# Hybrid gated block in fp32 on one core: eight late down-weight sums, late up-weight splits, and squares behind the embedding copies

## Chip, cores and metric

One core of a Trainium2 chip runs one launch of a hand-written kernel. The metric is the device time of that launch in microseconds (us), as the median of several runs. Engines are named as in the profile: PE is TensorE, DVE is VectorE, ACT is ScalarE, POOL is GpSimd, SP is SyncE (it only issues DMAs here). Line numbers L... are those of the kernel before, unless a row of the changed kernel is shown.

## What is computed

A decoder block with batch 1, sequence 512, model width 1024, one layer, all in float32:

```python
h = rms_norm(x, g_mix_pre); z = h @ w_in              # 1024 -> 512 + 1024 + 1024 + 2048
u_pool, u_rx, u_rg, gates = split(z); gate_pool, gate_rnn = sigmoid(gates)
y_pool = pool_mixer(u_pool, pool_w, pool_scale) @ w_pool_out
y_rnn = rg_lru_branch(u_rx, u_rg, ...) @ w_rg_out
x = x + rms_norm((gate_pool * y_pool + gate_rnn * y_rnn) @ w_o, g_mix_post)

up = rms_norm(x, g_ffn_pre) @ w_up                    # 1024 -> 2 * 3072
hid = gelu(causal_dwconv(up[..., :3072], w, b)) * up[..., 3072:]
x = x + rms_norm(hid @ w_down, g_ffn_post)            # 3072 -> 1024

ple_gate = sigmoid(rms_norm(x, g_ple_gate) @ w_ple_gate)
ple = rms_norm(p @ w_ple_proj, g_ple_post)            # the embedding product, 256 -> 1024
out = x + ple_gate * ple
```

The change lies between the product with `w_o` and the product with `w_down`.

## The kernel before

**Products.** A float32 product is made of three matmuls (`mm3`, L222 to L224): each operand is split into a rounded part `hi` and a remainder `lo`, and hi·hi, hi·lo and lo·hi are added in PSUM, a memory of eight banks of 128 x 512. A weight block of 128 x 1024 is loaded by SP into one of six `raw` buffers; ACT rounds it (the *cast*, L195 or L455), DVE subtracts (the *remainder*, L191), and `split` does both. The buffer is free for the next load when the remainder is done. `weight` asks for blocks four products ahead (`AHEAD`).

**Seven products in place of eight.** The products with `w_rg_out`, `w_o`, `w_up` and `w_down` are done over 2 x 2 blocks (two halves of the tokens, two halves of the sum or of the columns) by a scheme of seven products, numbered 1 to 7 and called *forms*. Sums and differences of activation blocks are made by DVE. Those of weight blocks are mostly made in DRAM, by accumulating DMAs that POOL issues (`sum_in_dram`, L303 to L311): for the down weights 48 of them, in 24 blocks that are read back later as `wdsum`. Of the up weights only the first two pairs do that; from the third pair on DVE adds the blocks (`up_form`, L387).

**Stages around the change.** Tokens go in four tiles of 128. First comes the product with `w_o` (forms in the order 1, 2, 5, 6, 3, 7, 4; L1070 to L1096): as a form's bank is done, ACT copies it or DVE subtracts it (L1078, L1086, L1088, L1091). Behind each come `x2_sum` and `x2_out`, which normalise a token tile (two *squares* on ACT with a running sum, L489, a power on POOL, two multiplies on DVE), store `x2` to DRAM and make the inputs of the up product, `h2_tile` transposes them on PE, and ACT and DVE split them again.

Second, `ple_tile(t)` makes the embedding product of token tile t in two banks; DVE copies the one (L833), ACT the other (L834), SP stores both. `ple_norm(t)` takes two squares of the result. Third comes the up product. Its 24 column blocks are done in 12 pairs of one gate block and one value block. Pair 0 is done plainly, with blocks 11, 21, 12, 22 (`up_plain`), pairs 1 to 11 by `up_product(f, p)` in the order 1, 3, 6, 2, 7, 5, 4 (form 3 of pair p comes after form 1 of pair p+1). Their banks are `zb` for forms 1, 6 and 7, `gb` and `ub` for the gate and the value, `db` for form 5. After each of forms 1, 5, 6 and 7 ACT copies the bank with or without a sign (L1125, L1128, L1130, L1132, L1133), and PE goes on accumulating onto what was written. Last comes the down product (`down_product`, 7 forms of 6 blocks, L1337 on), with transposes and the embedding gate behind it.

**What sets the order.** PE runs in program order. On the other engines a list scheduler orders instructions by data and by priority: `urgent()` raises it, `tc.high_priority(offset)` too. `behind(ins, name)` adds an edge that only fixes an order on the engine, without a wait. An instruction waits at the head of its engine's queue, and all behind it wait with it. `paced[0]` is the last copy of ACT; `sum_in_dram(sums, n, paced[0])` makes the next n sums wait for it, so that they are spread over the up product. Before, two sums follow each of forms 1, 6 and 5 of pairs 2 to 9 (from `SUMS_FROM`, `SUMS_AFTER`, `SUMS_EACH`): six per pair, 48 in all.

Of the kernel before, what the change touches and what calls it, by code (L numbers as in the profile page):

```python
# [12 lines left out]
ALU = mybir.AluOpType  # L13
# [35 lines left out]

UP_SUMS = (1, 2)  # L50

SUMS_FROM, SUMS_AFTER, SUMS_EACH = 2, (1, 6, 5), 2


PLACES, PLACE_UP, PLACE_H2 = 64, 48, (1072, 46)
# [28 lines left out]
def block_kernel(  # L84
# [62 lines left out]
    def parts_of(n):  # L147

        return [wpool.tile([P, D], F32R, tag=t, name=nm(t))[:, :n] for t in ("hi", "lo")]
# [4 lines left out]
    def behind(ins, name):  # L154
        tc.add_manual_dep(
            ins.ins,
            name,
            mybir.DependencyInfo(mybir.DependencyClass.NoSync, mybir.DependencyReason.DATA),
            reason="order on the engine",
        )  # L160
# [46 lines left out]
    def row(a):  # L207
        return a.rearrange("p (a b) -> p a b", a=2)
# [178 lines left out]
    def up_form(p, f):  # L387

        b = blocks
        if p == 0:  # L390
            t = block(0, f)
        elif p in UP_SUMS:
            t = block(p, {1: 11, 2: 21, 3: 22}.get(f, f))
        elif f == 1:
            for k in (11, 12, 22, 21):
                b[p, k] = block(p, k)
            b[p, 0] = wpool.tile([P, 2, S], F32, tag="sum", name=nm("sum"), bufs=1)
            t = b[p, 11]
        elif f == 6:
            add(b[p, 0], b[p, 11], b[p, 12])  # L400
            t = b[p, 11]
            add(t, b[p, 0], b[p, 22])
        elif f == 7:
            t = b[p, 12]
            add(t, t, b[p, 22])
        elif f == 4:
            t = b[p, 21]
            add(t, b[p, 11], t)
        else:
            t = b[p, {2: 21, 3: 22, 5: 0}[f]]  # L410
        hi, lo = (v.rearrange("p (j c) -> p j c", j=2) for v in parts_of(D))
        split(hi, lo, t)
        if p == 0 and PLAIN.index(f) > 1:
            behind(last_copy[0], h2f_done[0])
        if p == 0 and PLAIN.index(f) > 0:
            behind(last_sub[0], h2n_done[1])
        if p == 1 and f != 1:
            behind(last_copy[0], h2_done[0])
        if (p, f) == (1, 4):
            behind(last_sub[0], hid_done[0])  # L420
        if p > 2 and f == 6:
            behind(last_copy[0], z_done[0])
        ready["up", p, f] = (hi, lo)

    def prep(key):
        if key[0] == "up" and key not in parts:
# [392 lines left out]

    rp = {}  # L820
    h2n_done, h2f_done, z_copied, hid_done, summed = {}, [None], [None], [None], {}

    def ple_tile(t):
        pair = []
        for h in range(2):
            w = weight(("wpp", h))
            ps = bank()
            for k in range(2):
                a = pick(pq[k], t * P, (t + 1) * P)
                mm3(ps, a, pick(w, k * S, (k + 1) * S), k == 0, k == 1)  # L830
            pair.append(ps)
        outs = [slot(), slot()]
        V.tensor_copy(row(outs[0]), back(pair[0]))  # L833
        ACT.copy(row(outs[1]), back(pair[1]))  # L834
        for h, o in enumerate(outs):
            nc.sync.dma_start(pled[t * P : (t + 1) * P, h * S : (h + 1) * S], o)
        return outs

    def ple_norm(t, outs):
        s = rstd_of(outs, in_order=False)  # L840
        rp[t] = const.tile([P, 1], F32, tag=f"rp{t}", name=f"rp{t}")
        V.tensor_copy(rp[t], s)

# [33 lines left out]
    def o_form(f):  # L877

        h11, h12, h21, h22 = (halves(mq[k], b) if k < len(mq) else None for b in range(2) for k in range(2))
        v = {1: h11, 2: h12, 4: h22}.get(f)  # L880
        if f in (5, 7):
            od[f] = quad("C", F32)[:, 0:2, :].rearrange("p a (b c) -> p (a b) c", b=2)
        if f == 5:
            v = od[5]
            behind(V.tensor_tensor(v, h21, h22, ALU.subtract), last_low[0])
        elif f == 6:
            v = od[5]
            V.tensor_tensor(v, v, h11, ALU.subtract)
        elif f == 3:
            v = od[5]  # L890
            V.tensor_tensor(v, v, h12, ALU.add)
        elif f == 7:
            v = od[7]
            V.tensor_tensor(v, h11, h21, ALU.subtract)
        of[f] = quad("A").rearrange("p (s a) (b c) -> p s (a b) c", s=2, b=2)
        split(of[f][:, 0], of[f][:, 1], v)
        if f in (2, 5):
            behind(last_copy[0], z_copied[0])

    def o_lhs(f, k, i):  # L900
        v = of[f][:, :, k, i * P : (i + 1) * P]
# [168 lines left out]
    for n, f in enumerate(SERIAL):  # L1070
        banks = {1: oz, 2: o11, 5: od5, 6: oz, 3: o12, 7: oz, 4: oz}[f]
        last = f == SERIAL[-1]
        for q in product("wo", o_lhs, f, banks, f in (1, 5), tail=2 if f in (1, 6, 3, 7, 4) else 0):
            if q in (0, 2) and n + 1 < len(SERIAL) and SERIAL[n + 1] not in of:
                o_form(SERIAL[n + 1])
            if f == 1:
                with urgent():
                    z_copied[0] = ACT.copy(o11[q - 2], oz[q - 2]).ins.name  # L1078
            if f == 7 and q == 2:
                x2_norm(1, (o11[1], o12[1]))  # L1080
            if last and q == 2:
                h2_tile(0)
        for i in range(2):
            with urgent():
                if f == 5:
                    ACT.copy(o5[:, i], od5[i])  # L1086
                elif f == 6:
                    V.tensor_tensor(o12[i], o5[:, i], oz[i], ALU.subtract)  # L1088
                elif f == 7:
                    with urgent():  # L1090
                        V.tensor_tensor(o5[:, i], o5[:, i], oz[i], ALU.subtract)  # L1091
        if f == 3:
            x2_norm(0, (o11[0], o12[0]))
            for h in range(2):
                h2h.append(token_halves())
                h2l.append(token_halves())  # L1096
# [15 lines left out]
    def up_product(f, p):  # L1112
        for i in range(2):
            w = weight(("up", p, f))
            if f == 1 and p > 1:
                gb[i] = bank()
                if p == 2 and i == 0:
                    PE.matmul(gb[i], w[0][:, 0, :P], w[0][:, 0, :], start=True, stop=True)
            o = {1: zb, 6: zb, 7: zb, 2: gb, 4: gb, 3: ub, 5: {0: db, 1: db}}[f][i]
            a = HALF if f == 4 or (f, i) == (5, 1) else 0  # L1120
            products(o[:, a : a + HALF], w, i, forms[f], f in (1, 5))
            z = zb[i][:, :HALF]
            with urgent():
                if f == 1 and p > 1:
                    paced[0] = ACT.copy(gb[i][:, :HALF], z).ins.name  # L1125
                elif (f, i) == (5, 1):
                    q5[p] = temp()
                    paced[0] = ACT.copy(q5[p], o).ins.name  # L1128
                elif f == 6:
                    paced[0] = ACT.activation(ub[i][:, :HALF], z, AF.Identity, scale=-1.0).ins.name  # L1130
                elif f == 7:
                    ACT.copy(gb[i][:, HALF:], z)  # L1132
                    z_done[0] = ACT.activation(ub[i][:, HALF:], z, AF.Identity, scale=-1.0).ins.name  # L1133
# [12 lines left out]
    def hidden(j, pu, q):  # L1146
# [8 lines left out]
            pu = hid[j]  # L1155
        hid_done[0] = V.tensor_tensor(hid[j], act_g[j], pu, ALU.mult).ins.name

    for t in range(NT):
        with tc.high_priority(offset=3 * URGENT):
            outs = ple_tile(t)  # L1160
        if t == 1:
            h2_tile(1)
            x2_out(2, h2_done[0])
            x2_sum(3, (oz[1], o5[:, 1]))
            x2_out(3)
            ple_norm(0, outs0)
        if t == 0:
            outs0 = outs
        else:
            ple_norm(t, outs)  # L1170
    for kind, n in O_AFTER:
        if kind == "tr":
            h2_tile(n)
# [53 lines left out]
    for p in range(1, NPAIR + 1):  # L1227
        for q, f in seven(p):
            if (q, f) == (1, 1):
                continue  # L1230
            up_product(f, q)
            if f in SUMS_AFTER and p >= SUMS_FROM:
                sum_in_dram(down_sums, SUMS_EACH, paced[0])
            if f == 4:
                for i in range(2):
                    gated_half(2 * q + i, gb[i])
            if f == 3:
                for i in range(2):
                    hidden(2 * q + i, ub[i], q5[q][:, i * HALF : (i + 1) * HALF])
# [94 lines left out]
        )  # L1334
    nq = [None, None]

    for _ in down_product(1, zd, True, tail=2):  # L1337
        pass
    for i in range(2):
        with urgent():  # L1340
            ACT.copy(c11[i], zd[i])
    for _ in down_product(2, c11, False, head=2):
        pass
    for _ in down_product(5, dd, True):
# [146 lines left out]
```

## Time and profile before

| what | value |
|---|---|
| runs | 707.17, 707.8, 709.17 us |
| median | 707.8 us |
| the profiled execution, by its own time | 711.61 us |
| its span in the profile | 709.8 us |
| its mean granted TensorE clock | 0.997 |
| moved by DMA, over the span | 175.72 MB, 248 GB/s mean |

The profiled execution is 3.8 us longer than the median of the other runs; durations are taken from it. How to read its rows: a row of the timeline has the start in us from the start of the span, the duration of one, engine, line, operation, out<-in with the shape, and in brackets how long the engine had been idle and for what. A row that ends in x2 or x3 stands for as many in succession, and its duration is their sum. A row of a group has the busy time in all and the mean of one in ns. A row of windows has the stretch, then the busy us of the engines, the granted clock, the busy share of the DMA engines and GB/s. PE is busy while a matmul is in its pipeline.

### The profile page before, as it was taken

The numbers are of one execution on the slowest core, as the hardware profiler recorded it, in microseconds if no ns is written. First come the engines' busy times: TensorE is split into PE (matmuls) and PEld (weight loads), VectorE is DVE, ScalarE is ACT, GpSimd is POOL, SyncE is SP. The second block draws the span as 40 slices with busy tenths as digits, with TensorE's granted clock in tenths as the row PEclk, the third lists the DMA queues.
The fourth block names the chain that finished last, engine by engine and source line by source line (L and its number), as shares of the span: only waits on it lengthen the run. The fifth ranks groups of instructions, "written<-read, shape, count | busy, mean of one in ns | idle before, by whom it ended". The sixth has DMA issues, their size and how long they took to land.

```text
span 709.8 us, 11608 instructions
## 1 busy us (share of the span) xinstructions
PE 695.8 (98%) x4423; PEld 639.9 (90%) x4423; DVE 592.3 (83%) x772; ACT 454.7 (64%) x693; POOL 94.7 (13%) x123
## 2 busy tenths in 40 slices
PE   9999999999999999999989999999999999999997
PEld 8888888888888998889989999999999888888886
DVE  5698745999759898787979999997999999789972
ACT  6757789835447565579846776665768766665631
POOL 0311321412000000111013222221300000000100
PEclk9999999999999999999999999999999999999999
DMA  8999899999997988764478999997977676868111
GB/s 310 412 304 278 244 237 254 244 289 239 280 336 276 320 328 327 260 239 147 133 244 250 262 309 251 321 233 262 252 202 243 196 265 216 285 212 257 68 61 60
DMA packets 67289, 175.72 MB, mean 248 GB/s; under 512 B 6049, under 2 KB 6689, under 8 KB 66849
## 3 DMA queue, kind: packets, MB, share of 16 engines
q1 hardware_dynamic: 49808, 124.64, 50.1%
q0 software_dynamic: 17280, 50.34, 30.1%
q8 instruction: 35, 0.57, 0.3%
q14 instruction: 22, 0.17, 0.1%
q10 hardware_dynamic: 144, 0.00, 0.0%
HBM read 162.37 MB, written 62.91 MB: 317 GB/s over the span
## 4 chain that ended last, share of the span: by engine, by line
PE 70%; DVE 12%; DMA 8%; ACT 6%; issue 3%; POOL 0%; SPq 0%; DVEq 0%; ACTq 0%
PE ps L222 22%; PE ps L224 22%; PE ps L223 22%; DMA raw<-in_w_up_dram 4%; PE ps L563 3%; DVE lo L191 3%; ACT m L166 1%; DVE m L701 1%; DMA parts<-hi 1%; ACT t L166 1%; DVE m L628 1%; ACT hi L195 1%; DVE t L772 1%; PE ps L672 1%; DMA raw<-in_w_pool_out_dram 1%
## 5 line engine op out<-in xcount | busy, mean ns | idle before, releaser
L191 DVE TENSOR_TENSOR lo<-raw,hi 128x1024 fp32r<-128x1024 f32 (+2 forms) x199 | 230.9, 1187 | 51.1 <-ACT hi L455 30.3
L222 PE MATMUL ps<-A,hi 128*128 128x256 f32 (+1 forms) x672 | 213.0, 317 | 3.7 <-ACT ps L1130 2.8
L223 PE MATMUL ps<-A,hi 128*128 128x256 f32 (+1 forms) x672 | 212.3, 316 | 0.0
L224 PE MATMUL ps<-A,lo 128*128 128x256 f32 (+1 forms) x672 | 212.2, 316 | 0.0
L455 ACT CAST hi<-raw 128x1024 fp32r<-128x1024 f32 (+1 forms) x118 | 118.1, 1012 | 59.1 <-PE ps L224 27.6
L222 PEld LDWEIGHTS ps<-A,hi 128*128 128x128 f32 x672 | 129.0, 192 | 12.4 <-ACT ps L1130 3.0
L224 PEld LDWEIGHTS ps<-A,lo 128*128 128x128 f32 x672 | 129.1, 192 | 6.9
L223 PEld LDWEIGHTS ps<-A,hi 128*128 128x128 f32 x672 | 129.0, 192 | 6.7
L222 PE MATMUL ps<-C,hi 128*128 128x256 f32 x376 | 103.7, 276 | 2.0 <-ACT m L834 2.0
L223 PE MATMUL ps<-C,hi 128*128 128x256 f32 x376 | 103.3, 275 | 0.8 <-DVE C L191 0.8
L224 PE MATMUL ps<-C,lo 128*128 128x256 f32 x376 | 103.2, 274 | 0.0
L195 ACT CAST hi<-raw 128x1024 fp32r<-128x1024 f32 x78 | 80.4, 1051 | 33.2 <-PE ps L223 16.2
L222 PE MATMUL ps<-hi,A 128*128 128x512 f32 x224 | 85.2, 380 | 1.1 <-issue 1.1
L223 PE MATMUL ps<-lo,A 128*128 128x512 f32 x224 | 84.9, 379 | 0.0
L224 PE MATMUL ps<-hi,A 128*128 128x512 f32 x224 | 84.9, 379 | 0.0
L222 PEld LDWEIGHTS ps<-C,hi 128*128 128x128 f32 x376 | 71.8, 191 | 2.7 <-ACT m L834 2.3
L223 PEld LDWEIGHTS ps<-C,hi 128*128 128x128 f32 x376 | 71.8, 191 | 1.2 <-DVE C L191 1.1
L224 PEld LDWEIGHTS ps<-C,lo 128*128 128x128 f32 x376 | 71.8, 191 | 0.0
L484 POOL TENSOR_TENSOR s<-s,mhalf 128x1 f32<-128x1 f32 (+1 forms) x21 | 14.8, 707 | 319.2 <-DVE s L500 297.3
L222 PEld LDWEIGHTS ps<-hi,A 128*128 128x128 f32 x224 | 42.3, 189 | 7.4 <-issue 1.5
L307 POOL DMA_DIRECT2D wdsum<-in_w_down_dram x36 | 33.3, 1086 | 113.1 <-ACT ps L1125 50.1
L224 PEld LDWEIGHTS ps<-hi,A 128*128 128x128 f32 x224 | 42.3, 189 | 6.0
(202 smaller groups left out, 1069.3 us busy)
## 6 DMA issues: line engine op xcount, KB each, us to landing
raw<-in_w_up_dram SPq DMA_DIRECT2D x46, 512.0 KB, 7.2
wdsum<-in_w_down_dram POOLq DMA_DIRECT2D x36, 512.0 KB, 9.0
raw<-in_w_in_dram SPq DMA_DIRECT2D x32, 512.0 KB, 8.7
raw<-wdsum SPq DMA_DIRECT2D x24, 512.0 KB, 4.4
raw<-in_w_down_dram SPq DMA_DIRECT2D x18, 512.0 KB, 3.9
wosum<-in_w_o_dram POOLq DMA_DIRECT2D x12, 512.0 KB, 8.5
wdsum<-wdsum POOLq DMA_DIRECT2D x12, 512.0 KB, 7.9
raw<-wosum SPq DMA_DIRECT2D x8, 512.0 KB, 6.3
```

The lines of the kernel that those rows point to most:

```text
L166: ins = ACT.activation(o, i, func, **kw)
L191: return V.tensor_tensor(o, a, b, ALU.subtract)
L195: last_copy[0] = ACT.copy(hi, src)
L222: PE.matmul(o, ah, bh, start=start, stop=False, **kw)
L223: PE.matmul(o, ah, bl, start=False, stop=False, **kw)
L224: PE.matmul(o, al, bh, start=False, stop=stop, **kw)
L307: ins = nc.gpsimd.dma_start(o, i, **kw)
L455: ins = ACT.copy(hi, raw)
L484: last_pow[0] = nc.gpsimd.tensor_tensor(y, v, mhalf[:, :n], ALU.pow).ins.name
L563: PE.matmul(rx[m], a[:, o : o + P], turns(b), start=k == 0 and i == 0, stop=k == KD - 1 and i == 2)
L628: return V.tensor_tensor(row(o), back(ps), row(rb), ALU.mult)
L672: PE.matmul(ps, bd[pr, a, o], turns(b[pr]), start=i == 0, stop=i == 2)
```

## The change

Five edits, all in the order of work; no arithmetic changes.

1. **Sums of the down weights.** After form 1 two, after forms 6 and 5 one each: four per pair, from pair 2 on as long as there are pairs (2 to 11). Four more wait for the last product of hidden values (`hid_done`), and the last four for the copies of the first form of the down product.
2. **Late up weights.** The splits of blocks 12 and 22 of pair 0 are kept in a list and issued after `h2_tile(1)`, behind the remainders of the second token tile.
3. **Squares of the embeddings.** All four `ple_norm` come after all four `ple_tile`, and their squares go behind the copy L834 of the last tile (`ple_done`). The squares in `x2_out(3)` go behind the copy of tile 2.
4. **Form 3 of the up product**, pairs 2 to 11: the cast of its weight goes behind both form-6 copies of its own pair (`z6_done`).
5. **Product with `w_o`**: the remainders of the activations of forms 7 and 4 go behind the two subtractions after form 6 (`o_done`).

```diff
-SUMS_FROM, SUMS_AFTER, SUMS_EACH = 2, (1, 6, 5), 2
+SUMS_FROM, SUMS_AFTER, SUMS_DOWN = 2, {1: 2, 6: 1, 5: 1}, 4
...
+        if p == 0 and f in PLAIN[2:]:
+            late.append((f, t))
+            return
         hi, lo = (v.rearrange("p (j c) -> p j c", j=2) for v in parts_of(D))
         split(hi, lo, t)
-        if p == 0 and PLAIN.index(f) > 1:
-            behind(last_copy[0], h2f_done[0])
-        if p == 0 and PLAIN.index(f) > 0:
+        if (p, f) == (0, PLAIN[1]):
             behind(last_sub[0], h2n_done[1])
...
+        if p > 1 and f == 3:
+            behind(last_copy[0], z6_done[p])
         ready["up", p, f] = (hi, lo)
+
+    def late_splits():
+        for f, t in late:
+            hi, lo = (v.rearrange("p (j c) -> p j c", j=2) for v in parts_of(D))
+            low = last_low[0]
+            split(hi, lo, t)
+            behind(last_copy[0], h2f_done[0])
+            behind(last_sub[0], low)
+            ready["up", 0, f] = (hi, lo)
...
-        ACT.copy(row(outs[1]), back(pair[1]))
+        ple_done[0] = ACT.copy(row(outs[1]), back(pair[1])).ins.name
...
-    def ple_norm(t, outs):
-        s = rstd_of(outs, in_order=False)
+    def ple_norm(t, outs, after):
+        s = rstd_of(outs, in_order=False, after=after)
...
+        if f in (7, 4):
+            behind(last_sub[0], o_done[f == 4])
...
-                    V.tensor_tensor(o12[i], o5[:, i], oz[i], ALU.subtract)
+                    o_done[i] = V.tensor_tensor(o12[i], o5[:, i], oz[i], ALU.subtract).ins.name
...
-                    paced[0] = ACT.activation(ub[i][:, :HALF], z, AF.Identity, scale=-1.0).ins.name
+                    z6_done[p] = paced[0] = ACT.activation(ub[i][:, :HALF], z, AF.Identity, scale=-1.0).ins.name
...
+        ple_outs.append(outs)
         if t == 1:
             h2_tile(1)
+            late_splits()
             x2_out(2, h2_done[0])
             x2_sum(3, (oz[1], o5[:, 1]))
-            x2_out(3)
-            ple_norm(0, outs0)
-        if t == 0:
-            outs0 = outs
-        else:
-            ple_norm(t, outs)
+        if t == 2:
+            x2_out(3, ple_done[0])
+    for t in range(NT):
+        ple_norm(t, ple_outs[t], ple_done[0])
...
-                sum_in_dram(down_sums, SUMS_EACH, paced[0])
+                sum_in_dram(down_sums, SUMS_AFTER[f], paced[0])
...
+    sum_in_dram(down_sums, SUMS_DOWN, hid_done[0])
     for _ in down_product(1, zd, True, tail=2):
         pass
     for i in range(2):
         with urgent():
-            ACT.copy(c11[i], zd[i])
+            paced[0] = ACT.copy(c11[i], zd[i]).ins.name
+    sum_in_dram(down_sums, None, paced[0])
```

The edits move instructions on ACT at three places. Row names are the kernel's tiles with running numbers, and line numbers of the changed kernel are 13 to 15 higher.

At the embedding copies of token tiles 2 and 3, ACT before (L489 with `m455`, `m456` are the squares of x2 of the last token tile, with `m560` to `m565` those of the first two embeddings; L834 are the copies that free a bank, `C504` and `C506` casts of the last token tile, `hi612` the cast of an up weight):

```order
L195 CAST hi612_3228<-raw611_3226 128x1024
L489 ACTIVATE rb_134,s580_3133<-m455_2652 128x512
L489 ACTIVATE rb_134,s581_3135<-m456_2654 128x512
L489 ACTIVATE rb_134,s586_3145<-m560_3059 128x512
L489 ACTIVATE rb_134,s587_3147<-m561_3060 128x512
L834 COPY m597_3180<-ps595_3172 128x512
L834 COPY m605_3210<-ps603_3202 128x512
L489 ACTIVATE rb_134,s590_3155<-m564_3079 128x512
L195 CAST C504_2881<-ps615_3281 128x4x128
L195 CAST C506_2883<-ps618_3292 128x4x128
L489 ACTIVATE rb_134,s591_3157<-m565_3080 128x512
```

and in the changed kernel, where L847 is the copy, L501 the square, and `hi564` and `hi566` are the two late up weights:

```order
L195 CAST hi564_3095<-raw552_3033 128x1024
L847 COPY m583_3146<-ps581_3138 128x512
L195 CAST hi566_3099<-raw554_3042 128x1024
L195 CAST hi612_3228<-raw611_3226 128x1024
L501 ACTIVATE rb_134,s584_3153<-m455_2652 128x512
L501 ACTIVATE rb_134,s585_3155<-m456_2654 128x512
L847 COPY m593_3180<-ps591_3172 128x512
L195 CAST C504_2881<-ps615_3281 128x4x128
L195 CAST C506_2883<-ps618_3292 128x4x128
L501 ACTIVATE rb_134,s594_3185<-m556_3051 128x512
L1042 COPY m616_3288<-ps615_3281 128x2x128
```

The first copy now stands ahead of all these squares and the second behind only those of x2, two casts of weights have come in, and the squares of the embeddings (from `m556` on) follow the casts of the last token tile.

At form 6 of pair 1, ACT before (`A548` is the input of form 3 of the up product, `ps621` and `ps622` the value banks that L1130 writes, the casts with `hi` are of up weights: `hi653` of form 1 of pair 2, `hi656` of form 3 of pair 1, `hi660` and `hi663` of forms 6 and 2 of pair 2):

```order
L195 CAST A548_3029<-m645_3551 128x512
L195 CAST A548_3029<-m646_3553 128x512
L195 CAST hi650_3569<-raw649_3567 128x1024
L195 CAST hi653_3601<-raw652_3599 128x1024
L195 CAST hi656_3631<-raw655_3629 128x1024
L1130 ACTIVATE ps621_3303<-ps549_3030 128x256
L1130 ACTIVATE ps622_3316<-ps550_3031 128x256
L195 CAST hi660_3663<-raw659_3661 128x1024
L195 CAST hi663_3697<-raw662_3695 128x1024
L1128 COPY t658_3659<-ps551_3032 128x512
```

and in the changed kernel, with L1145 for L1130:

```order
L195 CAST A548_3029<-m645_3551 128x512
L195 CAST hi650_3569<-raw649_3567 128x1024
L195 CAST hi653_3601<-raw652_3599 128x1024
L195 CAST A548_3029<-m646_3553 128x512
L195 CAST hi656_3631<-raw655_3629 128x1024
L195 CAST hi660_3663<-raw659_3661 128x1024
L1145 ACTIVATE ps621_3303<-ps549_3030 128x256
L1145 ACTIVATE ps622_3316<-ps550_3031 128x256
L195 CAST hi663_3697<-raw662_3695 128x1024
L1143 COPY t658_3659<-ps551_3032 128x512
```

One more cast, `hi660`, stands ahead of the two copies, and half of the cast of `A548` goes behind two casts of weights.

At form 6 of pair 2, ACT before (`hi686` is the weight of form 3 of that pair, `hi683` that of form 1 of the next):

```order
L195 CAST hi683_3849<-raw678_3840 128x1024
L1130 ACTIVATE ps621_3303<-ps549_3030 128x256
L195 CAST hi686_3879<-raw685_3877 128x1024
L1130 ACTIVATE ps622_3316<-ps550_3031 128x256
L1132 COPY ps670_3741<-ps549_3030 128x256
L1133 ACTIVATE ps621_3303<-ps549_3030 128x256
```

and in the changed kernel:

```order
L195 CAST hi683_3848<-raw678_3839 128x1024
L1145 ACTIVATE ps621_3303<-ps549_3030 128x256
L1145 ACTIVATE ps622_3316<-ps550_3031 128x256
L195 CAST hi686_3878<-raw685_3876 128x1024
L1147 COPY ps670_3741<-ps549_3030 128x256
L1148 ACTIVATE ps621_3303<-ps549_3030 128x256
```

The cast that stood between the two copies now stands behind them; the same edge is set in every pair from 2 to 11.

More of the change, by code (lines that the diff above doesn't have):

```diff
@@ L821, in block_kernel @@
     h2n_done, h2f_done, z_copied, hid_done, summed = {}, [None], [None], [None], {}
+    z6_done, o_done, ple_done, late = {}, {}, {}, []
     def ple_tile(t):
@@ L1156, in hidden @@
         hid_done[0] = V.tensor_tensor(hid[j], act_g[j], pu, ALU.mult).ins.name
+    ple_outs = []
     for t in range(NT):
```

## The prediction, made before the changed kernel was run

> **What bounds the kernel now.** The page first: which engine is full.
>
> ```profile
> PE 695.8 (98%) x4423; PEld 639.9 (90%) x4423; DVE 592.3 (83%) x772; ACT 454.7 (64%) x693; POOL 94.7 (13%) x123
> ```
>
> TensorE is busy for 695.8 of 709.8 us and its matmuls are untouched by the change, so all that can be won is in its few waits. The view of waits, TensorE's own, from 270 to 520 us, lists them whole (waited for: us in total, times, longest):
>
> ```profile
> PE ps L222 <- ACT ps L1130: 2.8, 1, 2.8
> PE ps L222 <- ACT m L834: 2.0, 1, 2.0
> PE ps L222 <- issue: 1.1, 1, 1.1
> PE ps L222 <- ACT ps L1125: 0.8, 1, 0.8
> PE ps L223 <- DVE C L191: 0.8, 1, 0.8
> ```
>
> Five stops, 7.6 us. Two come with a hidden price, which the windows show (columns of the first: PE, PEld, DVE, ACT, POOL busy, clock, DMA share, GB/s; of the others PE alone, clock, DMA):
>
> ```profile
> 330.00:340.00 10.00, 10.00 (x92) 10.00 (x91) 10.00 (x15) 7.23 (x13) 0.00 (x0) 1.00 0.46 157
> 360.00:370.00 10.00, 7.17 (x64) 1.00 0.66 225
> 370.00:380.00 10.00, 10.00 (x76) 0.83 0.54 185
> 372.00:373.00 1.00, 1.00 (x6) 0.50 0.93 324
> 322.00:323.00 1.00, 1.00 (x11) 1.00 0.84 311
> ```
>
> At full clock 92 of the 256-wide matmuls pass in 10 us, 0.11 us each. After the 2.8 us stop the granted clock is 0.50 and 76 pass in the next ten: 16 are missing, 1.7 us. After the 2.0 us stop (322:323) it is 1.00, nothing more is lost. [...]
>
> **The change part by part.** Three edits lie in front of 330 us.
>
> ```profile
> 283.84 0.45 PE L222 MATMUL ps<-hi,A 128*128 128x512 f32 x1 [1.14 <-issue]
> 281.91 1.23 DVE L191 TENSOR_TENSOR A<-C,A 128x1024 fp32r<-128x1024 f32 x1 [0.21 <-ACT A L195]
> 283.05 1.29 DVE L1088 TENSOR_TENSOR ps<-sum,ps 128x512 f32<-128x512 f32 x2
> 312.62 0.38 PE L223 MATMUL ps<-C,hi 128*128 128x256 f32 x1 [0.78 <-DVE C L191]
> 308.49 3.47 DVE L191 TENSOR_TENSOR lo<-raw,hi 128x1024 fp32r<-128x1024 f32 x3
> 321.05 0.38 PE L222 MATMUL ps<-C,hi 128*128 128x256 f32 x1 [2.04 <-ACT m L834]
> 319.05 0.63 ACT L489 ACTIVATE rb<-m 128x512 f32<-128x512 f32 x1
> 320.43 1.05 ACT L834 COPY m<-ps 128x512 f32<-128x512 f32 x2
> ```
>
> First, the subtraction at L1088, which the product after it accumulates onto, moves ahead of two remainders of 1.23 us that are not yet due: its first half can run when its bank is done, before 282.7, and the 1.14 us stop goes (1.2 with the restart). Second, two of the three remainders at 308.49 are the late up weights (1.13 us each); put behind the second token tile they let that tile's own remainder start 2.3 us earlier, more than the 0.78 us wait (0.9). Third, the squares of the embedding norms (0.73 us each on ACT, with the read of the sum) go behind the copies that free the banks, and the copy of tile 2 now stands before the squares of the last token tile: the 2.04 us wait goes (2.1). Together 4.2 us.
>
> ```profile
> 310.35 1.97 SPq L379 DMA_DIRECT2D raw<-up1sum  x3
> ```
>
> On SP these three loads, issued back to back now, come apart: four stores of embeddings and two of x go between them. Their products start after 330, and the loads of the whole run take 7.2 us or less in the median (row below), so I cost this at nothing; without that cover it would be the wait of one load. POOL keeps its order; its sums only wait for later copies of ACT.
>
> I don't expect TensorE to keep them. The squares are not fewer, only later, and the next token tile's casts stand behind them:
>
> ```profile
> 323.30 1.28 DVE L191 TENSOR_TENSOR C<-ps,C 128x512 fp32r<-128x512 f32 x2
> 327.72 1.07 ACT L195 CAST C<-ps 128x512 fp32r<-128x512 f32 x2
> 339.03 0.36 ACT L1185 COPY ps<-ps 128x256 f32<-128x256 f32 x1 [1.56 <-DVE t L1140]
> 345.39 2.94 ACT L195 CAST hi<-raw 128x1024 fp32r<-128x1024 f32 x3
> 348.24 0.64 ACT L1130 ACTIVATE ps<-ps 128x256 f32<-128x256 f32 x2
> 348.82 0.28 PE L222 MATMUL ps<-A,hi 128*128 128x256 f32 x1
> ```
>
> Today four squares lie between the remainder of token tile 2 (323.30) and the casts of tile 3 (327.72); in the new order six, 1.5 us more. Adding the rows along ACT and DVE in the new order, that remainder comes 2.2 us earlier (1.2 from the first stop, the rest from the two remainders moved away), so the casts come only about half a us earlier, while TensorE wants them 4.2 us earlier: it stops there for some 2 us, and for about 0.6 us before that on banks that the copies between those squares free. DVE is full behind them (10.00 in 330:340), and there one remainder of a weight now stands ahead of the second step of L1140, for which L1185 waits at 339.03: its lead stays near 0.5 us. Last, ahead of L1130 now stand four casts instead of three. They take 0.95 each (2.85 from 345.39 to 348.24), so L1130 starts at 348.24 + 0.95 - 0.5 = 348.7, ends 0.3 later, and TensorE, which starts the product behind it at 348.82 now, starts it near 349.0. So by 349 the 4.2 us are gone, to within 0.2 us; I put this stage at 0. Its ends: without any lead on ACT 349.2 + 0.3, a loss of 0.7; with the lead of all three stops, a gain of 4.2 less 0.95, 3.2.
>
> The part with a lasting effect is a line that is easily missed: the cast of a later weight (form 3, used five products on) is put behind both copies of form 6.
>
> ```profile
> 358.45 1.23 DVE L385 TENSOR_TENSOR sum<-raw,raw 128x1024 f32<-128x1024 f32 x1 [2.01 <-DMA raw<-in_w_up_dram]
> 360.26 1.22 DVE L191 TENSOR_TENSOR lo<-raw,hi 128x1024 fp32r<-128x1024 f32 x1
> 361.54 6.87 DMA raw<-in_w_up_dram
> 363.70 0.37 ACT L1130 ACTIVATE ps<-ps 128x256 f32<-128x256 f32 x1
> 364.38 0.69 DVE L1149 TENSOR_TENSOR h<-ps,t 128x512 f32<-128x512 f32 x1
> 368.48 1.04 ACT L195 CAST hi<-raw 128x1024 fp32r<-128x1024 f32 x1 [4.41 <-DMA raw<-in_w_up_dram]
> 369.43 0.37 ACT L1130 ACTIVATE ps<-ps 128x256 f32<-128x256 f32 x1
> 369.85 0.38 PE L222 MATMUL ps<-A,hi 128*128 128x256 f32 x1 [2.83 <-ACT ps L1130]
> ```
>
> The remainder at 360.26 frees the buffer of a load of 6.87 us; the cast that waits for it (368.48) stands between the two copies of L1130, and TensorE waits for the second. In the new order that copy needs only DVE's L1149 (364.38 + 0.69), so it can run at 365.1, 1.9 us before TensorE stops at 367.0 (369.85 - 2.83). Besides, the remainder goes ahead of the sum that waits 2.01 us for DMA, so the load leaves earlier too. What is queued behind the waiting cast on ACT are then L1132 and L1133. Even with the load as late as today they would follow at 369.4, and the product that needs them starts 12 and then 24 matmuls after 367.0, at 371. So this stop falls whole: 2.8, and the 1.7 of half clock.
>
> The sums: six issues in each pair from the second to the ninth become four up to the eleventh, and eight move behind the up products.
>
> ```profile
> 430.10:448.80 18.70, 18.70 (x170) 18.70 (x169) 17.61 (x19) 12.42 (x21) 4.07 (x6) 1.00 1.10 293
> 560.00:640.00 80.00, 80.00 (x373) 70.05 (x372) 72.38 (x68) 52.92 (x61) 1.41 (x1) 1.00 0.75 245
> 473.20 18.09 DMA raw<-in_w_up_dram
> 498.86 0.38 PE L222 MATMUL ps<-A,hi 128*128 128x256 f32 x1 [0.83 <-ACT ps L1125]
> raw<-in_w_up_dram SPq DMA_DIRECT2D x46, 512.0 KB, 7.2
> raw<-wdsum SPq DMA_DIRECT2D x24, 512.0 KB, 4.4
> ```
>
> The DMA engines are full in a pair (1.10), and one load took 18.09 us against a median of 7.2; it ends in the 0.83 us stop. A pair moves four loads and six sums; counting a sum as two loads (read and write), 16 become 12, the share falls to about 0.8, and I take the stop as gone: 0.9. The eight sums go where the share is 0.75 and TensorE never waits. A piece there is 12 matmuls, 373 in 80 us or 2.6 us, and loads go four pieces ahead, 10.3 us, against 4.4: that cover hides them.
>
> The sum against the profiled execution's own time, 711.6: 0 + 4.5 + 0.9 = 5.4, so 706.2. That execution lies 3.8 us above the median of 707.8. If all of the 3.8 is the cost of profiling, the median falls to 702.4; if all of it is stops that plain runs lack, only 1.6 is left and the time is 706.2. The three runs are 2.0 us apart, about the 1.7 of half clock, so I take that the median run lacks the half clock and has the rest: 707.8 - 3.7 = **704.1**.
>
> **The rivals.** (a) The early gain is kept, because ACT gets through its squares sooner than I add up: up to 3.2 us more, about 701. For it: ACT is busy for only 7.23 of 10 there; against it: DVE's 10.00. (b) The stops at 367 and 498 belong to late loads, and the loads stay late: the wait goes from L1130 to the product that uses the weight, or plain runs hardly had them. Then 1 us or less is won, 707. For it: both chains run through a DMA wait, and plain runs are 3.8 us faster; against: 1.9 us of cover. (c) The half clock comes back: the new stops, 0.6 and 2 us, lie within some 4 us, and a stop of 2.8 paid where one of 2.0 did not. That costs 1.7: 705.8. [...] (d) Slower: the sums in the down stage. They share the engines with the 24 loads of sums; if such a load takes 18.09 us as the one at 473.20 did, it outlasts the 10.3 us ahead by 7.8, and TensorE stops for it: 711.9. It decides from 10.3 us on, and only once here do I expect it even then. Against: 0.75, and sums that come in two groups of four.
>
> **How the numbers follow.** My case 0.45, at 702.5 to 705.5 by itself; (a) 0.16; (b) 0.16; (c) 0.12; (d) 0.11. What a measurement here can tell from no change is 0.3%, 2.1 us: faster means under 705.7. My case and (a) are that, and a third of (c): 0.65. Same: (b), the rest of (c): 0.24. Slower: (d): 0.11. The range from 700.5 to 708.5 holds all but (d) and the far end of (a).
>
> **What would show it.** In the new profile: no wait at L1088 and none of the second tile's C; a wait of 1 to 2 us on ACT casts near 327 and one before 349 on what is L1145 there (L1130 now); none at 367, clock 1.00 in 370:380; DMA share under 1 in the pairs; no stop from 550 to 650. I am wrong if TensorE is more than 1 us ahead at 354, or if it stops behind a raw load.

## The result, and the profile after

Eleven runs of each kernel: before 708.17 us in the median (707.17 to 709.62), the changed kernel 705.26 us (704.80 to 708.11). The ratio is 0.9962 with an interval of 0.9950 to 0.9974: 2.9 us less, 1.8 to 3.5. The profiled executions lie further apart, 711.61 and 706.08 us by their own times.

The page of the changed kernel, first part, the line of TensorE:

```profile
PE 693.9 (99%) x4423; PEld 638.9 (91%) x4423; DVE 592.0 (84%) x772; ACT 454.1 (64%) x693; POOL 95.9 (14%) x123
```

The same matmuls, 1.9 us less busy time (1.7 of it the half clock that is not there), and a shorter span around them. TensorE's waits from 270 to 720 us in the changed kernel (waited for: us in total, times, longest):

```profile
PE ps L222 <- ACT C L195: 1.1, 1, 1.1
PE ps L222 <- ACT ps L1145: 0.7, 1, 0.7
PE ps L222 <- ACT m L1042: 0.7, 2, 0.6
PE ps L222 <- ACT ps L1201: 0.5, 1, 0.5
PE ps L223 <- DVE C L191: 0.3, 1, 0.3
```

None of the five stops of before is left at its place; six smaller ones stand elsewhere, 3.3 us against 7.6. The timeline of TensorE shows where the four longest are (start, us, line, operation, idle before and its releaser; L1042, L1145 and L1201 are L1027, L1130 and L1185 of the kernel before):

```profile
323.70 0.38 PE L222 MATMUL ps<-C,hi 128*128 128x256 f32 x1 [0.55 <-ACT m L1042]
328.13 0.38 PE L222 MATMUL ps<-C,hi 128*128 128x256 f32 x1 [1.05 <-ACT C L195]
341.55 0.38 PE L222 MATMUL ps<-A,hi 128*128 128x256 f32 x1 [0.48 <-ACT ps L1201]
349.26 0.38 PE L222 MATMUL ps<-A,hi 128*128 128x256 f32 x1 [0.75 <-ACT ps L1145]
```

All lie before 350. Behind that TensorE runs through; the windows at the place of the old 2.8 us stop, in a pair and in the down stage (PE, PEld, DVE, ACT, POOL, clock, DMA share, GB/s):

```profile
360.00:370.00 10.00, 10.00 (x92) 10.00 (x91) 9.03 (x11) 5.14 (x10) 2.09 (x3) 1.00 0.94 316
370.00:380.00 10.00, 10.00 (x92) 10.00 (x92) 9.60 (x11) 8.05 (x12) 1.98 (x3) 1.00 0.61 200
430.10:448.80 18.70, 18.70 (x170) 18.70 (x169) 17.54 (x20) 12.48 (x20) 2.96 (x5) 1.00 0.74 225
560.00:640.00 80.00, 80.00 (x373) 70.16 (x371) 70.85 (x71) 52.27 (x62) 6.11 (x6) 1.00 0.91 289
```

In a pair the DMA share is 0.74 (1.10 before; about 0.8 was said, an estimate that counts a sum as two loads). The down stage carries the eight sums at 0.91 (0.75 before) without a stop here; the loads of sums take twice as long in the median as the 4.4 us of before, but still less than the 10.3 us by which they go ahead:

```profile
raw<-wdsum SPq DMA_DIRECT2D x24, 512.0 KB, 8.5
```

ACT and DVE around 360, where the two copies of form 6 (now L1145) follow each other:

```profile
357.13 1.22 DVE L191 TENSOR_TENSOR lo<-raw,hi 128x1024 fp32r<-128x1024 f32 x1
359.07 1.23 DVE L385 TENSOR_TENSOR sum<-raw,raw 128x1024 f32<-128x1024 f32 x1
...
362.53 0.36 ACT L1145 ACTIVATE ps<-ps 128x256 f32<-128x256 f32 x1
363.99 0.37 ACT L1145 ACTIVATE ps<-ps 128x256 f32<-128x256 f32 x1 [1.09 <-DVE h L1164]
364.46 1.06 ACT L195 CAST hi<-raw 128x1024 fp32r<-128x1024 f32 x1
```

Two things differ from before. The second copy no longer stands behind a cast. And that cast, 4 us earlier than the one of before (368.48), does not wait for its load at all, since on DVE the remainder that frees the buffer now precedes the sum that waits for DMA. Which of the two ended the stop, this profile alone cannot say.

**A measure without the start.** Profiled executions differ before any edit acts: ACT's first copy in the product with `w_o` began between 263.5 and 268.2 us in all profiles here. So profiles are compared below by the time from that copy to ACT's first copy in the down product, called the *stretch*. In the changed kernel the two rows (count, duration, first and last start) are

```profile
L1093 ACT COPY ps<-ps x2: 570/570/570, 264.9 to 267.5; 128x512 f32<-128x512 f32 x2
L1358 ACT COPY ps<-ps x2: 570/570/570, 558.6 to 561.2; 128x512 f32<-128x512 f32 x2
```

so its stretch is 293.7 us. In the first profile of before it is 564.4 - 264.6 = 299.8, by the same two copies (line numbers of the changed kernel are 12 to 17 higher than those of before, not 13 to 15):

```profile
L1078 ACT COPY ps<-ps x2: 570/570/570, 264.6 to 267.2; 128x512 f32<-128x512 f32 x2
L1341 ACT COPY ps<-ps x2: 570/570/570, 564.4 to 567.0; 128x512 f32<-128x512 f32 x2
```

### The profile page after: what moved, and what is told of

Same layout as the page of the kernel before. It is cut to its first block, busy times and chain, and to the rows that moved or that the text cites. A ratio compares the mean times of both kernels' runs of the same rounds, so it can differ in the third digit from the quotient of the medians.

```text
span 704.1 us, 11599 instructions
## 1 busy us (share of the span) xinstructions
PE 693.9 (99%) x4423; PEld 638.9 (91%) x4423; DVE 592.0 (84%) x772; ACT 454.1 (64%) x693; POOL 95.9 (14%) x123
## 4 chain that ended last, share of the span: by engine, by line
PE 73%; DVE 13%; ACT 6%; DMA 3%; issue 3%; POOL 1%; SPq 0%; DVEq 0%; ACTq 0%
PE ps L222 23%; PE ps L224 23%; PE ps L223 23%; DVE lo L191 3%; PE ps L575 3%; ACT m L166 2%; DVE m L713 1%; DMA parts<-hi 1%; ACT t L166 1%; ACT hi L195 1%; POOL s L496 1%; DVE m L640 1%; DVE t L784 1%; ACT rb L501 1%; PE ps L684 1%
## 5 line engine op out<-in xcount | busy, mean ns | idle before, releaser
L224 PEld LDWEIGHTS ps<-hi,A 128*128 128x128 f32 x224 | 42.4, 189 | 6.0
L223 PEld LDWEIGHTS ps<-lo,A 128*128 128x128 f32 x224 | 42.4, 189 | 5.8
```

The lines of the kernel that those rows point to most:

```text
L223: PE.matmul(o, ah, bl, start=False, stop=False, **kw)
L224: PE.matmul(o, al, bh, start=False, stop=stop, **kw)
```

## The experiments

They were run in three series, each with runs of the kernel before of its own (medians 708.60, 708.12 and 708.93 us). A ratio in the tables is to those of the same series.

**First: the parts, each alone.** `edge_only` is the kernel before with the line on the casts:

```diff
+        if p > 1 and f == 3:
+            behind(last_copy[0], z6_done[p])
```

> The kernel before with one line of the change: the cast of form 3's weight goes behind both form-6 copies. My theory: the 2.8 us stop before the second form-6 copy falls whole, and what half clock comes with it; the 0.8 us stop behind a raw load near 499 stays. Plain runs 2.8 us shorter than before (2.0 to 4.5). Rival 1, plain runs hardly have this stop: less than 0.7 us shorter. Rival 2, the load stays late and the wait goes on to the product that uses the weight: no stop at the copy, but one of 1 us or more within 10 us behind it.

`pace_only` is the kernel before with the pacing alone:

```diff
-SUMS_FROM, SUMS_AFTER, SUMS_EACH = 2, (1, 6, 5), 2
+SUMS_FROM, SUMS_AFTER, SUMS_DOWN = 2, {1: 2, 6: 1, 5: 1}, 4
...
+    sum_in_dram(down_sums, SUMS_DOWN, hid_done[0])
     for _ in down_product(1, zd, True, tail=2):
...
+    sum_in_dram(down_sums, None, paced[0])
```

> The kernel before with the pacing of the sums alone: four per pair up to the eleventh, eight in the down stage. My theory: only the 0.8 us stop near 499 falls, the stop at the second form-6 copy stays, since the cast before it still waits for its load: 0.9 us shorter than before (0 to 1.5). Rival 1: fewer sums bring the load of 6.87 us in so early that the stop at the copy goes too: 2 us or more shorter. Rival 2, the sums in the down stage make a down load late: a stop of TensorE between 550 and 650, not shorter than before.

`early_only` is the changed kernel without that line and with the old pacing, so that the three early edits are left:

> The kernel before with the three early edits alone (late up weights, squares of the embeddings, remainders of the product with w_o). My theory: the three early stops, 4.0 us, fall and come back as others before 350; at most 0.7 us is left there, and the stop at the form-6 copy, which waits for a load, takes that too: within 0.7 us of before. Rival: what is gained early is kept: 0.7 to 3 us shorter than before.

`no_edge` is the changed kernel without the line on the casts:

> The changed kernel without the line that puts the cast of form 3's weight behind both form-6 copies. My theory: the stop at the second form-6 copy is back, 1.5 to 3 us in its profile, and the time is 2 us or more above the changed kernel, 707 to 708. Rival: the pacing of the sums alone had taken that stop away: within 0.7 us of the changed kernel's 705.3, no stop at the copy.

| run | median, us | ratio to before | interval | stretch in its profile, us |
|---|---|---|---|---|
| edge_only | 705.89 | 0.9947 | 0.9926 to 0.9968 | 294.8 |
| pace_only | 708.86 | 0.9996 | 0.9972 to 1.0020 | 297.4 |
| early_only | 705.68 | 0.9958 | 0.9937 to 0.9979 | 294.7 |
| no_edge | 705.71 | 0.9955 | 0.9936 to 0.9973 | 293.7 |

The line alone wins 2.7 us in the median, as my theory had it. Its profile shows the mechanism of the prediction by itself: on DVE the sum that waits still stands ahead of the remainder, the load is still late for the cast, and the second copy no longer waits for either.

```profile
357.49 1.23 DVE L385 TENSOR_TENSOR sum<-raw,raw 128x1024 f32<-128x1024 f32 x1 [2.17 <-DMA raw<-in_w_up_dram]
359.30 1.22 DVE L191 TENSOR_TENSOR lo<-raw,hi 128x1024 fp32r<-128x1024 f32 x1
...
364.20 0.37 ACT L1133 ACTIVATE ps<-ps 128x256 f32<-128x256 f32 x1 [1.08 <-DVE h L1152]
366.26 1.05 ACT L195 CAST hi<-raw 128x1024 fp32r<-128x1024 f32 x1 [1.70 <-DMA raw<-in_w_up_dram]
```

This profile starts the product with `w_o` 1.1 us earlier than the first of before, so the copy at 364.20 stands at 365.3 there; 365.1 was forecast.

The pacing alone wins nothing that can be told: its interval leaves room for 2.0 us less and 1.4 us more. But the early edits alone win as much as the line, and the changed kernel without the line loses nothing: both of these expectations of mine missed. The rivals beside them had the times right, but not the reasons (an early gain that is kept, and the pacing). The gains don't add up; two parts remove the same thing. In `early_only` and `no_edge` the cast still stands between the two copies, yet there is no stop: the load it waits for is early. The program order shows why. The early edits changed, by way of the scheduler, the order of some DVE instructions as much as 30 us behind them, among them the two in question: the remainder of form 5 of pair 2 now precedes the first sum of pair 3.

**Second: that swap alone, and both undone.** `order_only` is the kernel before with this swap and nothing else; the cast stays between the copies:

```diff
+        if f == 5:
+            low5[p] = last_low[0]
...
         elif f == 6:
-            add(b[p, 0], b[p, 11], b[p, 12])
+            ins = V.tensor_tensor(b[p, 0], b[p, 11], b[p, 12], ALU.add)
+            if p == 3:
+                behind(ins, low5[2])
```

> The kernel before with one swap on DVE and nothing else: the remainder of form 5 of pair 2 goes ahead of the first sum of pair 3, which waits 2 us for DMA. The cast of form 3's weight still stands between the two form-6 copies. Theory 1 (from the runs without that line): the stop belongs to this order, which sends the load of form 3's weight late; with the swap the load lands 3 us earlier and the stop of 2.8 us is gone or under 0.5: 2 to 4 us shorter than before, as with the line on the casts alone. Theory 2 (as I forecast): only the line on the casts lifts the stop; here 1.5 us of it stay and under 1 us is won.

`both_undone` is the changed kernel without the line on the casts and with the swap turned back (`behind(low5[2], ins.ins.name)`, `low5` now the remainder itself); a few DVE instructions around the two move with it:

> The changed kernel without the line on the casts and with the old order of that remainder and that sum on DVE; early edits and pacing stay. Theory 1: the stop at the second form-6 copy is back with 2 to 3 us, and half clock behind it in some runs: 2 to 3.5 us above the changed kernel, 707.5 to 708.8, so the rest of the change is worth under 1 us. Theory 2, the early edits and the pacing have a gain of their own: within 1 us of the changed kernel.

`before_again` is the kernel before, unchanged:

> The kernel before once more, for a second profile of it. If the stop at the second form-6 copy is a matter of order, it is there again with 2 to 3 us and half clock behind it; if it was chance of one execution, under 1 us. The start of the products with w_o, 264.6 in the first profile, shows how far executions differ before any part of the change.

| run | median, us | ratio to before | interval | stretch, us |
|---|---|---|---|---|
| order_only | 705.87 | 0.9955 | 0.9938 to 0.9972 | 295.0 |
| both_undone | 708.50 | 0.9996 | 0.9976 to 1.0015 | 295.9 |
| before_again | 709.21 (one run) | | | 296.8 |

The swap alone gives the whole gain; with swap and line both undone the changed kernel is as fast as the kernel before (to about 0.2%), early edits and pacing notwithstanding. The timeline of DVE and ACT in `order_only`:

```profile
357.72 1.21 DVE L191 TENSOR_TENSOR lo<-raw,hi 128x1024 fp32r<-128x1024 f32 x1
360.30 1.23 DVE L400 TENSOR_TENSOR sum<-raw,raw 128x1024 f32<-128x1024 f32 x1 [0.70 <-DMA raw<-in_w_up_dram]
...
365.38 1.07 ACT L195 CAST hi<-raw 128x1024 fp32r<-128x1024 f32 x1 [1.23 <-DMA raw<-in_w_up_dram]
366.34 0.36 ACT L1134 ACTIVATE ps<-ps 128x256 f32<-128x256 f32 x1
```

The remainder runs at 357.72 in place of 360.26, and the cast between the copies at 365.38 in place of 368.48, so the second copy (366.34) is done before TensorE comes to it. TensorE is late itself in this profile, by a half clock behind 321 (0.50 in 323:324). `no_edge` has none there (1.00 in all its windows); its cast at 364.93 still waits 1.72 us for the load, the second copy runs at 365.88, and TensorE does not stop either. In `both_undone` the old picture is back:

```profile
358.18 1.23 DVE L400 TENSOR_TENSOR sum<-raw,raw 128x1024 f32<-128x1024 f32 x1 [1.27 <-DMA raw<-in_w_up_dram]
359.98 1.22 DVE L191 TENSOR_TENSOR lo<-raw,hi 128x1024 fp32r<-128x1024 f32 x1
...
367.06 1.04 ACT L195 CAST hi<-raw 128x1024 fp32r<-128x1024 f32 x1 [4.80 <-DMA raw<-in_w_up_dram]
368.01 0.37 ACT L1147 ACTIVATE ps<-ps 128x256 f32<-128x256 f32 x1
...
368.43 0.38 PE L222 MATMUL ps<-A,hi 128*128 128x256 f32 x1 [1.99 <-ACT ps L1147]
```

The second profile of before has the stop too, by its timeline,

```profile
370.51 0.38 PE L222 MATMUL ps<-A,hi 128*128 128x256 f32 x1 [3.00 <-ACT ps L1130]
```

and no half clock behind it, by its windows (columns as above):

```profile
370.00:380.00 10.00, 9.49 (x85) 9.49 (x86) 8.59 (x8) 7.78 (x14) 2.65 (x4) 1.00 0.65 217
```

So the stop belongs to the order; the half clock of the first profile does not. The stop near 499 comes and goes: this profile has none there, and `edge_only`, with the old pacing, has one again:

```profile
492.77 0.38 PE L222 MATMUL ps<-A,hi 128*128 128x256 f32 x1 [0.81 <-ACT ps L1128]
```

Of all profiles here two of the five with the old pacing have it, and none of the nine with fewer sums per pair. So the new pacing may well take it away; but 0.8 us in two of five executions is 0.3 us on average, too little to be seen in `pace_only`.

**Third: can the early gain be kept?** `cast_back` puts one cast more behind the copies of form 6, in pair 1:

```diff
+        if (p, f) == (2, 6):
+            behind(last_copy[0], z6_done[1])
```

> The changed kernel with the cast of form 6 of pair 2 behind the form-6 copies of pair 1, nothing else. Theory: the 0.75 us stop before these copies was that cast of 0.95 us, and goes whole; the others stay: 0.75 us below the changed kernel, 704.5, too little for the interval, so the stop in its profile decides. Rival: the stop stays, since what ACT does before is late.

`squares_late` puts all squares of the embeddings behind the casts of the last token tile:

```diff
-    for t in range(NT):
-        ple_norm(t, ple_outs[t], ple_done[0])
     for kind, n in O_AFTER:
...
+    for t in range(NT):
+        ple_norm(t, ple_outs[t], h2_done[0])
     for f in PLAIN:
```

> The changed kernel with all squares of the embeddings behind the casts of the last token tile, nothing else. Theory: the stops on the casts and before them go (2.1 us), but the squares stand in ACT's way further on, so the stop before the form-6 copies of pair 1 grows from 0.75 to 2 us or more: 0 to 1 us below the changed kernel, 704.3 to 705.3. Rival: they fit into idle time of ACT there: 703.2 or less.

`both` has these two edits together:

> The changed kernel with two orders more: all squares of the embeddings go behind the casts of the last token tile, and the cast of form 6 of pair 2 behind the form-6 copies of pair 1. Theory: the stops behind the casts of the last tile (1.05 and 0.35), before them (0.55 and 0.16) and before the form-6 copies (0.75) shrink to under 1 us in all; 1 to 2 us below the changed kernel, 703.3 to 704.3. Rival: DVE and ACT are full from 330 to 350, the squares only come back there: within 0.5 us of the changed kernel.

`best` splits the squares, four ahead of the copies of token tile 2 and four behind the casts of tile 3, and puts two casts behind the copies of form 6:

```diff
+        if (p, f) in ((2, 6), (2, 1)):
+            behind(last_copy[0], z6_done[1])
...
         if kind == "tr":
             h2_tile(n)
+            with urgent():
+                for t in (2 * n - 4, 2 * n - 3):
+                    ple_norm(t, ple_outs[t], h2_done[0])
+            if n == 2:
+                for ins in h2f_copies[-4:]:
+                    behind(ins, last_sq[0])
```

> The changed kernel with three orders more: the squares of the first two embeddings go into the 2.7 us in which ACT waits before the copies of token tile 2, the other four behind the casts of token tile 3; the casts of form 1 and form 6 of pair 2 go behind the form-6 copies of pair 1. Theory: of the five stops between 320 and 350 (3.3 us) under 1 us stays, and the time is 2 to 3 us below the changed kernel: 702.3 to 703.3, under the run with all squares late (703.8). Rival: DVE, full there, sets the pace: 703.8 or more.

| run | median, us | ratio to before | interval | stretch, us |
|---|---|---|---|---|
| cast_back | 705.71 | 0.9949 | 0.9927 to 0.9971 | 293.9 |
| squares_late | 703.36 | 0.9916 | 0.9893 to 0.9939 | 291.5 |
| both | 703.78 | 0.9934 | 0.9909 to 0.9959 | 291.5 |
| best | 703.84 | 0.9921 | 0.9896 to 0.9946 | 292.1 |

`cast_back` wins nothing that can be told (0.75 us was expected): its stop before the copies of form 6 shrinks from 0.75 to 0.3 us, and one of 0.38 stands a little later. `squares_late` is the fastest here, 2.35 us below `cast_back` in the same series, with an interval that lies below that of the changed kernel: more than I expected, though short of the rival. `both` comes out as expected. The waits of TensorE in `squares_late`, all of them from 260 to 740 us:

```profile
PE ps L222 <- ACT ps L1145: 1.6, 1, 1.6
PE ps L222 <- ACT ps L1201: 0.2, 1, 0.2
```

and the two rows of its stretch:

```profile
L1093 ACT COPY ps<-ps x2: 570/570/570, 264.2 to 266.7; 128x512 f32<-128x512 f32 x2
L1358 ACT COPY ps<-ps x2: 570/570/570, 555.7 to 558.3; 128x512 f32<-128x512 f32 x2
```

Two stops, 1.8 us, in place of six with 3.3; the stretch is 2.2 us shorter. The squares come back, as the grown stop before L1145 shows, but not in full. The finer division in `best` is no better than this one edit; its time is the 703.8 of the rival, but that DVE sets the pace there is not shown.

**Fourth: the slower case of the prediction.** `down18` leaves 18 sums for the down stage in place of eight:

```diff
-SUMS_FROM, SUMS_AFTER, SUMS_DOWN = 2, {1: 2, 6: 1, 5: 1}, 4
+SUMS_FROM, SUMS_AFTER, SUMS_DOWN = 2, {1: 1, 6: 1, 5: 1}, 4
```

> The changed kernel with 18 sums of down weights in the down stage in place of eight (three per pair before). My theory: the DMA engines fill up there, but the loads of sums stay within the 10.3 us by which they go ahead: within 0.7 us of the changed kernel, no stop from 550 to 650. Rival (the slower case of the prediction): a sum or its load is late for the form that reads it and TensorE stops between 580 and 640: 2 us or more above the changed kernel.

It takes 723.70 us, ratio 1.020 (1.0175 to 1.0226), 18 us above the changed kernel: my theory missed, the rival holds. The stops of TensorE in the down stage, by its timeline:

```profile
602.58 0.48 PE L223 MATMUL ps<-lo,A 128*128 128x512 f32 x1 [0.67 <-DVE lo L191]
604.39 0.48 PE L223 MATMUL ps<-lo,A 128*128 128x512 f32 x1 [0.24 <-DVE lo L191]
622.26 0.77 PE L222 MATMUL ps<-hi,A 128*128 128x512 f32 x1 [13.94 <-DVE ps L1372]
```

the two longest rows of the chain of waits before the last of them (start, us, what), with the remainder that stands between them:

```profile
574.97 21.63 DMA raw<-wdsum
597.77 1.24 DVE lo L191
599.03 18.95 DMA raw<-in_w_down_dram
```

and the windows:

```profile
600.00:620.00 20.00, 7.41 (x32) 5.51 (x30) 10.52 (x10) 9.41 (x11) 0.00 (x0) 0.83 1.10 265
620.00:640.00 20.00, 17.74 (x72) 15.23 (x73) 14.60 (x15) 10.23 (x11) 0.00 (x0) 0.83 0.96 360
```

A load of a sum took 21.63 us, 11.3 more than the 10.3 us by which loads go ahead. The remainder that had waited for it then freed the buffer of the next load, which took 18.95 us more and landed at 618; behind its cast and another remainder stands L1372, for which TensorE waits. So one slow load behind another made the stop. The granted clock is 0.65 in 610:620 and 0.66 in 620:630, around the end of the stop: 72 matmuls pass in the 17.74 us of 620:640, where 95 in 20 us in the changed kernel would make 84, so 12 are missing, some 2.5 us. The three stops and the lower clock make some 17.3 of the 18 us.

## Why the prediction was right, and where it was not

**The forecast.** 704.1 us was said from 707.8, so 3.7 us less; measured are 2.9. The profiled executions differ by 5.5 us in their own times, and the sum against the profiled execution gave 5.4. That these two meet is partly luck: 0.9 of the 5.4 is a stop that the second profile of before does not have.

**The early edits at 0.** They held, by the mechanism that was given: the three early stops (3.96 us) are gone and come back as 3.3 us before 350: 0.55 and 0.16 on the banks that the copies between the squares free (0.6 was said), 1.05 and 0.35 at the casts of the last tile (2), 0.75 before L1145 (named without a size). The 0.48 before L1201 was not named; the prediction gave only the lead of that copy, about 0.5 us. TensorE starts the product behind L1145 at 349.26, which is 84.4 us behind ACT's first copy in the product with `w_o`; before it was 348.82 and 84.2, and 349.0 and 84.4 were forecast. So at this place nothing of the 4.2 us is left. `both_undone`, which keeps these edits and the pacing, is at 0.9996 of before.

**The stop at 367.** It went whole, with the cast behind both copies and clock 1.00 in 370:380, as forecast, and `edge_only` shows that the line does this alone. What I had not seen is that the change cures it twice. The prediction notes that the remainder goes ahead of the waiting sum "so the load leaves earlier too", and counts that as an aside; `order_only` shows that it is enough by itself, 0.9955. The line that I called the part with a lasting effect adds nothing that can be told once the swap is there (`no_edge` 0.9955 against 0.9962 for the whole change). So rival (b), loads that stay late, failed in two ways: in the changed kernel the load is no longer late, and in `edge_only`, where it still is, the cover holds and the wait does not go on to the product that uses the weight.

**The term that was wrong.** 0.9 us for the stop near 499, given to the pacing of the sums as if every execution had that stop. Two of five profiles with the old pacing have it, and the pacing alone measures 0.9996, so by these profiles it is worth some 0.3 us on average, which no run here can tell from noise. Without it the forecast for the median is 2.8, against 2.9 measured.

That this comes so near is partly luck, since the half clock, left out of the median, is not wholly absent there. Of the 70 runs of before in the three series, the 34 with a mean granted clock of 0.999 or more have a median of 707.53 us, the other 36 one of 709.29. The median lies between: about half of the runs lose clock somewhere, and their median is 1.8 us longer, about the 1.7 us of the half clock in the first profile. All eleven runs of the changed kernel are at 0.998 or more. So part of the 2.9 us is likely half clock that no longer follows a stop; how much, these runs do not show.

**The rivals.** (a) needed an early gain of up to 3.2 us; none of it is there at 349, but `squares_late` shows that 2 us can be had by placing the squares otherwise, so ACT does have the room that speaks for (a), only not in this order. (c) did not show: the clock of the changed kernel is 1.00 behind its new stops, also behind those of 0.55 and 1.05 us, 4.4 us apart; that stops close together pay like one long stop, no run here shows. (d) has the right mechanism and point: between eight and 18 sums a load outlasts the 10.3 us, though the price, 13.9 us at one stop, is far above the 7.8 us that I put on it, since a second slow load follows from the first.

## What to carry to other kernels

A stop that ends a chain through a DMA can have several independent cures: before one of them is credited, take each away alone and both together. When a scheduler places instructions, an edit can reorder a distant engine queue; compare the whole order, and look there for whatever frees the buffer of a late load. Work moved off a critical place must be followed to the next place where it stands in front of something awaited: here the squares' second place decided 2 us, and ten sums too many in a late stage cost 18.

## What the runs showed of the hardware

How long a stop must be before it costs half clock is not fixed in these profiles. The 2.0 us stop before 321 paid in two of five profiles that have it, `pace_only` (clock 0.50 in 322:323) and `order_only` (0.50 in 323:324), and not in the other three (1.00 in 320:330); the stop near 369 paid at 2.83 us in the first profile of before (0.50 in 372:373), and not at 3.00 (`before_again`), 2.15 (`pace_only`) or 1.99 us (`both_undone`), each with 1.00 in 370:380. The windows of `pace_only`, where the stop ends at 320.97:

```profile
320.00:330.00 10.00, 9.03 (x66) 9.03 (x67) 5.39 (x16) 8.68 (x25) 2.17 (x4) 0.83 0.46 160
322.00:323.00 1.00, 1.00 (x7) 1.00 (x7) 0.51 (x2) 1.00 (x4) 0.41 (x1) 0.50 0.95 352
```

and of `before_again`, after the same stop of 2.03 us:

```profile
320.00:330.00 10.00, 8.45 (x75) 8.46 (x76) 5.56 (x16) 9.59 (x27) 2.53 (x5) 1.00 0.48 164
```

In 9.03 us of busy time 66 matmuls passed, where at the rate of `before_again`, 75 in 8.45, it would be 80: 14 are missing, 1.6 us at 0.11 each. In `order_only` 61 passed in 8.50 us of the same stretch, again 14 fewer. So the same stop paid in some executions and not in others; the reason is not shown. A stop of 2 to 3 us cost its length here, and in three of these nine cases 1.6 to 1.7 us more.
